# A hybrid decoder layer on one core: later x and row loads, pauses for the bias table, fewer convolution taps beside the first output projection

## The chip, the core and the metric

One core of a Trainium2 chip runs the whole layer as a single launch. The core has TensorE (PE: matrix products, with weight loads shown as PEld), VectorE (DVE), ScalarE (ACT), GpSimd (POOL) and SyncE (SP). SyncE does no arithmetic in this kernel: it issues nearly all transfers, in the order of its own instruction list. Each engine takes its instructions in the order in which the build wrote them, and an instruction whose inputs or buffer are not ready holds up all behind it on that engine. The metric is the device time of one execution in microseconds; lower is better.

## The reference

A decoder layer for 2048 tokens of width 1024 in float32. An input projection gives queries, keys and values of a sliding-window attention (8 query heads, 2 key heads, window 128, a learned sink per head, a relative-position bias from a table of 32 buckets) and the input of a convolution group (gate, causal depthwise convolution of width 31, LayerNorm, swish, pointwise product). Both go through one output projection; a SwiGLU channel mixer follows. RMSNorms stand before and after each half.

```python
hn = rms_norm(h, mix_pre_g)
proj = hn @ w_in
attn_out = sliding_window_attention(q, k, v, attn_sinks, rel_bias)
conv_out = conformer_conv(u, conv_dw, conv_dw_b, conv_ln_g, conv_ln_b, w_conv_pw)
mixed = jnp.concatenate([attn_out, conv_out], axis=-1) @ w_out
h = h + rms_norm(mixed, mix_post_g)
hn = rms_norm(h, ffn_pre_g)
ff = (jax.nn.silu(hn @ w_gate) * (hn @ w_up)) @ w_down
h = h + rms_norm(ff, ffn_post_g)
```

## The kernel before

The tokens are cut into four tiles of 512, held transposed (128 features by 512 tokens). Each float32 operand is split into a high part, rounded to fp32r, and the low remainder, and each product of 128x128 by 128x512 is done three times (high by high, high by low, low by high). ScalarE makes the high parts, VectorE or GpSimd the low ones.

**Stages and labels.** A tile's name in the profile carries the label of the stage that made it: A is the input projections, B attention, C the convolution, U the folding of pointwise and output weights, W the output projection with its norm, H the operands for the channel mixer, F its gate and up products in Strassen form (two tiles of 512 at a time), G its down products, X the bias table. The order in time is A0 (tile 0), A1, A2, A3 with W0 beside it, W1, F and G of the first half, in G also W2 and W3, then F and G of the second half.

**Input projection** (`stage_a`). A tile has 14 units; a unit loads one weight block of 512 KB into one of two `raw` buffers (line 137), ScalarE splits off the high part (line 127), GpSimd (units under 6 of tile 0) or VectorE the low part (line 129 or 94), and TensorE makes 24 products (line 85). Tile 0 also writes the low parts to HBM (line 131), and later tiles read them back (line 126). Six buffers `w`, two per unit, hold split weights. After a unit a *hook* may run, which emits work for the next tile: `load_x` loads its transposed x in four transfers of 512 KB (line 253), `row_norms` loads its rows (line 267: four of 512 KB for tile 1, eight for tiles 2 and 3 together), squares and sums them on ScalarE (line 268) and computes the reciprocal root on VectorE and GpSimd (lines 153 to 156); `norm_x` spreads that factor over the features (four scalings of the identity on VectorE, four transposes at line 302, a copy at line 304); `split_x` scales and splits x. In tile 0 the hooks are `load_x` after unit 2, `row_norms` after unit 4, `norm_x` after units 8 and 10, `split_x` after 11 and 12. In tile 1 they are `load_x` after 0, `row_norms` after 2, then 7, 9, 10, 11; in tile 2 `load_x` after 0, then 4, 7 and 11. Tile 0 gets its own norm through a product with ones and transposes between its units 2 and 3.

**Lanes.** The program text is one run of main stages; each `yield c` says that work of about c us was emitted. A planner (`Lane.pump`) gives each side stage a credit of c times the lane's rate and lets it emit its own steps while the credit lasts. So `lb` (bias table X, then attention) runs at 0.8, the taps `lc` at 0.7, 1.1 and 0.4 for tiles 0, 1 and 2 and 0.1 for tile 3 until the first half's G stage, then 0.9; a tap costs 0.68. `lw` runs W0 at 1.7 while A3 is emitted. Taps are held from the end of W1 until the channel mixer's operands S0 are there.

**Order.** The build orders each engine's list by priority and by its own estimate of when inputs are ready, so an instruction with free inputs may be put well ahead of its place in the text. A manual dependency of class `NoSync` draws an edge between two instructions for this ordering and adds no semaphore. Taps (`stage_taps`, one VectorE instruction per tap, 30 a chunk after the first, 4 chunks a tile) carry such edges to the last main VectorE instruction and to products; `made["rows"]` holds the products emitted since the last paced VectorE instruction asked for a new list. The differences of the down weights (`stage_tsums`) have the same edge written out by hand.

**Bias table** (`stage_x`). It loads the table and a one-hot matrix, multiplies them (a product of 32 rows), writes the result to HBM, pauses, loads a skewed copy of it, pauses, and flips it with two products into the tile that attention's softmax adds.

**Output projection** (`stage_w`). Per group of two inputs and per half of the columns, four blocks of products; VectorE adds each to the sum `x@W` (line 94), except in the first group. A block yields 1.3 for its two units, and there are 32; the lead is 4 and the norm's steps add up to 24.

**Handover to the second half.** `stage_pre` of F makes products whose partial sums go to HBM (`keeps`, line 980), come back into `gb` (line 943) and are copied into PSUM by ScalarE (line 959) ahead of the second products. The tail of the first half's G stage reads `h_scr` into `chl` in the same stretch.

Of the kernel before, what the change touches and what calls it, by code (L numbers as in the profile page):

```python
# [18 lines left out]
ALU = mybir.AluOpType  # L19
# [6 lines left out]
P = 128  # L26
T = 512
# [10 lines left out]
def layer_kernel(ctx, tc, x, xT, cols, rows, sinks, relb, onehot, w_in, w_pw, w_out, w_gate, w_up, w_down, out):  # L38
    nc = tc.nc
# [7 lines left out]
    lab = ["X0"]  # L47
# [7 lines left out]
    def t_(tag, shape, dt=F32):  # L55
        return sb.tile(list(shape), dt, tag=tag, name=nm(tag), bufs=BUFS[tag])

    def f4(tag, shape=(P, D)):
        return t_(tag, shape)

    def f2(tag, shape=(P, T)):
        return t_(tag, shape)
# [4 lines left out]
    def sm(n, dt=F32):  # L67
        kind = "A" if lab[0][0] == "G" else lab[0][0]
        return sb.tile([P, 8], dt, tag="sm" + kind, name=nm("sm"), bufs=16)[:, 0:n]
# [11 lines left out]
    pace = {"main": None, "tied": None}  # L81
    made = {"rows": [], "at": 0, "new": True}

    def mat(*args, **kw):
        r = nc.tensor.matmul(*args, **kw)  # L85
        if made["new"]:
            made.update(rows=[], at=0, new=False)
        made["rows"].append(r.ins)
        return r


    def dve(op):
        def emit(*args, **kw):
            r = op(*args, **kw)  # L94
            if not paced[0]:
                pace["main"] = r.ins
            elif pace["main"] is not None and pace["main"] is not pace["tied"]:
                tc.add_manual_dep(
                    r.ins,
                    pace["main"].name,  # L100
                    mybir.DependencyInfo(mybir.DependencyClass.NoSync, mybir.DependencyReason.DATA),
                    reason="conv taps keep pace with the projections",
                )
                pace["tied"] = pace["main"]
            if paced[0] and made["rows"]:
                made["new"] = True
                tc.add_manual_dep(
                    r.ins,
                    made["rows"][min(made["at"], len(made["rows"]) - 1)].name,
                    mybir.DependencyInfo(mybir.DependencyClass.NoSync, mybir.DependencyReason.DATA),  # L110
                    reason="conv taps keep pace with the products",
                )
                made["at"] += TIE
            return r

        return emit

    stt = dve(nc.vector.scalar_tensor_tensor)
    vtt = dve(nc.vector.tensor_tensor)
# [54 lines left out]
    def after_first(first, r, how="NoSync"):  # L174
# [4 lines left out]
            reason="products of half the array stand together",  # L179
        )  # L180

    def three(o, pairs, first=True, last=True):
        n = 3 * len(pairs)
        i = 0
        for (sh, sl), (mh, ml) in pairs:
            for a, b in ((sh, mh), (sh, ml), (sl, mh)):
                mat(o, a, b, start=first and i == 0, stop=last and i == n - 1)
                i += 1
# [12 lines left out]
    for i in range(4):  # L201
        xt = f4("x", (P, 2, T))
# [43 lines left out]
    started = set()  # L246

    def load_x(t):
        lab[0] = f"A{t}"
        xs = []  # L250
        for i in range(4):
            xt = f4("x", (P, 2, T))
            nc.sync.dma_start(xt, xT[2 * i : 2 * i + 2, :, t * T : (t + 1) * T].rearrange("c p t -> p c t"))
            xs.append(xt)
        started.add(f"x{t}")
        return [xs]
# [3 lines left out]
    def row_norms(ts, tag):  # L260
        lab[0] = f"A{ts[0]}"
        n = 4 * len(ts)
        ssq = sm(n)
        for i in range(n):
            xt = f4(tag)
            r0 = ts[0] * T + i * P
            nc.sync.dma_start(xt, x[r0 : r0 + P])
            act(junk, xt, AF.Square, accum_out=ssq[:, i : i + 1])
        r = rsqrt(ssq, n, D)
        for j, t in enumerate(ts):  # L270
            rn[t] = r[:, 4 * j : 4 * j + 4]
# [405 lines left out]
    def stage_x():  # L677
        lab[0] = "X0"
        rel = cst.tile([32, 8], F32, name="rel")
        nc.sync.dma_start(rel, relb)  # L680
        oh = f2("fa", (P, 2 * P))
        nc.sync.dma_start(oh[0:32], onehot)
        pb = tr()
        mat(pb[0:8, 0 : 2 * P], rel, oh[0:32], start=True, stop=True)
        bs = f2("fa", (P, 2 * P))
        nc.vector.tensor_copy(bs[0:8], pb[0:8, 0 : 2 * P])
        b_scr = dr.tile([8, 2 * P], F32, name="b_scr")
        nc.sync.dma_start(b_scr, bs[0:8])
        yield 8
        lab[0] = "X0"  # L690
        flip = f2("fa", (P, P))
        nc.gpsimd.memset(flip, 0.0)
        nc.gpsimd.affine_select(
            out=flip, in_=flip, compare_op=ALU.not_equal, fill=1.0, base=1 - P, pattern=[[1, P]], channel_multiplier=1
        )
        up = t_("mb", (P, 8, P))
        nc.sync.dma_start(up, bass.AP(tensor=b_scr.tensor, offset=b_scr.offset, ap=[[1, P], [2 * P, 8], [1, P]]))
        yield 8
        lab[0] = "X0"
        t = t_("mb", (P, 8, P))  # L700
        for n in range(2):
            o = tr()
            mat(o, flip, up[:, 4 * n : 4 * n + 4].rearrange("p h k -> p (h k)"), start=True, stop=True)
            nc.vector.tensor_copy(t[:, 4 * n : 4 * n + 4].rearrange("p h k -> p (h k)"), o)
        bias.append(t)
        yield 0.1
# [412 lines left out]
    def stage_tsums(td):  # L1119
        L = "G0"  # L1120
        for pr in range(NF // 2):
            lab[0] = L
            wx = f4("wx", (P, 2, T))
            b = [wx[:, 0], wx[:, 1], f2("fc"), f2("fc")]
            for i, (f, n) in enumerate(((0, 0), (0, 1), (1, 0), (1, 1))):
                nc.gpsimd.dma_start(b[i], w_down[2 * pr + f, :, n * T : (n + 1) * T])
            yield 3.9
            b11, b12, b21, b22 = b
            for to, o, p_, q_ in ((0, b11, b12, b11), (2, b12, b22, b12), (1, b22, b22, b11), (3, b21, b21, b22)):
                lab[0] = L  # L1130
                r = vtt(o, p_, q_, ALU.subtract)
                tc.add_manual_dep(
                    r.ins,
                    made["rows"][-1].name,
                    mybir.DependencyInfo(mybir.DependencyClass.NoSync, mybir.DependencyReason.DATA),
                    reason="weight differences keep pace with the products",
                )
                nc.gpsimd.dma_start(td[to, pr], o)
                yield 0.25

# [179 lines left out]
    class Lane:  # L1320
        def __init__(self, rate, lag):
            self.lag = lag
            self.rate = rate
            self.rates = {}
            self.items = []
            self.credit = 0.0
            self.done = {}
            self.hold = lambda: False

        def add(self, name, gen, needs=None):  # L1330
            self.items.append((name, gen, needs))

        def pump(self, dt):
            if self.hold():
                return
            self.credit = min(self.credit + dt * self.rate, 6.0)
            while self.items and self.credit > 0:
                name, gen, needs = self.items[0]
                self.rate = self.rates.get(name, self.rate)
                if needs and not needs():  # L1340
                    self.credit = 0.0
                    return
                p0 = tc.cur_priority
                tc.cur_priority = p0 + self.lag
                paced[0] = self.lag > 0
                try:
                    c = next(gen)
                    self.credit = 0.0 if c is None else self.credit - c
                except StopIteration:
                    self.done[name] = clk[0]  # L1350
                    self.items.pop(0)
                tc.cur_priority = p0
                paced[0] = False
# [32 lines left out]
    lc = Lane(RC0, LC)  # L1386
    lw = Lane(RW0, 0)
# [4 lines left out]
    ld = Lane(2.0, 0)  # L1392
    lanes = [lb, lc, lu, lw, ld, lf, lh, lt]
    lh.rates = {"N1": 1.2, "S0": 0.8, "B21.2": 0.5, "S2": 0.8}
    lf.rates = {n: 0.6 for n in ("O0.1", "O0.3", "E0.1", "E0.3")} | {n: 1.2 for n in ("Y0", "Y1", "O2.1", "O2.3")}
    lc.rates = {"T0": RC0, "T1": RC1, "T2": RC2, "T3": RP}
    lw.rates = {"W0": RW0, "C2": RW, "W2": RW, "C3": RW, "W3": RW}

    def run(gen):
# [60 lines left out]
    keeps = [dr.tile([PRES[2 * i], P, T], F32, name=f"keeps{i}") for i in range(2)]  # L1460
# [7 lines left out]
    lh.add("S0", stage_h_sums(ws, ops), lambda: "N1" in lh.done)  # L1468
    run(stage_pre(ws, ops, mids[0], keeps[0], Q0))
    lt.add("TS", stage_tsums(td))  # L1470
    run(stage_p1(ws, ops, mids[0], keeps[0]))
    lt.until("TS")
# [80 lines left out]
```

## Time and profile before

| | us |
|---|---|
| median of 3 runs | 1951.76 |
| lowest and highest run | 1948.69, 1952.41 |
| the profiled execution, its own time | 1951.41 |
| its span in the trace | 1949.7 |
| mean granted TensorE clock | 0.993 |

The page gives busy time per engine and the costliest groups. A row of the list in order of time has start, duration, engine, line, operation, the tile written, the tiles read, a count of instructions merged, and in brackets the idle time before it with what ended it. A row of the waits has the waiting engine and group, the releaser, total us, times and longest. A row of the stretches has start and end, length, then busy us with counts for PE, PEld, DVE, ACT and POOL, the granted TensorE clock, the DMA engines' busy share and GB/s. Tile names carry the stage's label after @.

### The profile page before, as it was taken

What the parts mean: (1) busy time and instruction counts of PE and PEld (TensorE: products, weight loads), DVE (VectorE), ACT (ScalarE), POOL (GpSimd) and SP (SyncE); (2) the same over time, 40 slices, a digit from 0 to 9 for tenths busy, and PEclk for the clock granted to TensorE, in tenths of its full rate; (3) what the DMA queues carried; (4) which work ended last, traced back from release to release, by engine and by line L of the source; (5) the groups of instructions that cost most, each with busy time, mean ns of one, the idle gap of its engine ahead of it and who ended that gap; (6) DMA issues with size and microseconds to landing.
All of it is one profiled execution on the core that took longest, in us unless ns stands there. A gap on an engine that the chain in (4) does not pass through costs nothing.

```text
span 1949.7 us, 26646 instructions
## 1 busy us (share of the span) xinstructions
PE 1902.9 (98%) x8730; PEld 1537.4 (79%) x8730; DVE 1475.9 (76%) x2648; ACT 958.6 (49%) x1886; POOL 299.0 (15%) x427
## 2 busy tenths in 40 slices
PE   8999999999999999999999999998999999999997
PEld 6777777777777787788888788886788888888886
DVE  4999979995986998888579945578677776465557
ACT  5355455457658433334353555476534333345453
POOL 4011021011120111120000100000032333211003
PEclk9999999999999999999999999998999999999998
DMA  8787667667758767676477876769645443375663
GB/s 308 250 309 229 220 209 236 199 206 237 245 199 288 269 227 257 241 269 228 144 272 240 315 249 206 237 235 362 216 159 162 154 154 103 124 252 185 206 199 141
DMA packets 209578, 435.67 MB, mean 223 GB/s; under 512 B 21752, under 2 KB 39328, under 8 KB 209440
## 3 DMA queue, kind: packets, MB, share of 16 engines
q1 hardware_dynamic: 191648, 402.52, 61.8%
q0 software_dynamic: 7040, 23.07, 3.4%
q10 hardware_dynamic: 10752, 8.39, 1.3%
q8 instruction: 68, 1.11, 0.2%
q14 instruction: 70, 0.57, 0.1%
HBM read 323.26 MB, written 110.63 MB: 223 GB/s over the span
## 4 chain that ended last, share of the span: by engine, by line
PE 67%; DVE 15%; DMA 10%; issue 4%; ACT 2%; POOL 2%; SPq 1%; DVEq 0%; POOLq 0%; ACTq 0%
PE mm@F L85 30%; PE mm@G L85 17%; PE mm@A L85 8%; DVE fc@C L94 5%; PE mm@W L85 4%; PE tr@W L85 3%; PE tr@B L85 2%; DMA mids<-fa@F 2%; DVE w@F L94 1%; DMA keeps<-fa@F 1%; DVE chl@F L94 1%; DVE fa@F L94 1%; DMA w@W<-fold 1%; DMA gb@F<-keeps 1%; PE tr@B L504 1%
## 5 line engine op out<-in xcount | busy, mean ns | idle before, releaser
L94 DVE SCALAR_TENSOR_TENSOR fc@C<-glu@C,colt,fc@C 128x512 f32<-128x512 f32 x480 | 359.0, 762 | 2.7
L85 PE MATMUL mm@F<-hl@H,w@F 128*128 128x512 f32 x1056 | 261.1, 398 | 14.8 <-ACT mm@F L959 13.6
L85 PEld LDWEIGHTS mm@F<-hl@H,w@F 128*128 128x128 f32 x1056 | 201.1, 192 | 61.6 <-ACT mm@F L959 17.7
L85 PE MATMUL mm@G<-hl@G,hl@G 128*128 128x512 f32 x924 | 227.4, 393 | 1.8 <-DVE hl@G L94 1.8
L841 ACT ACTIVATE w@F<-chl@F 128x512 fp32r<-128x512 f32 x220 | 136.3, 626 | 186.3 <-PE mm@F L85 164.8
L85 PE MATMUL mm@A<-hl@A,w@A 128*128 128x512 f32 x840 | 207.9, 395 | 4.0 <-ACT w@A L127 2.1
L85 PEld LDWEIGHTS mm@G<-hl@G,hl@G 128*128 128x128 f32 x924 | 171.6, 188 | 38.3 <-DVE hl@G L94 2.6
L85 PE MATMUL mm@G<-w@G,hl@G 128*128 128x512 f32 x876 | 199.4, 389 | 0.0
L94 DVE TENSOR_TENSOR w@F<-chl@F,w@F 128x512 fp32r<-128x512 f32 x198 | 151.0, 765 | 59.9 <-ACT w@F L841 59.7
L85 PEld LDWEIGHTS mm@G<-w@G,hl@G 128*128 128x128 f32 x876 | 164.5, 188 | 34.1
L85 PEld LDWEIGHTS mm@A<-hl@A,w@A 128*128 128x128 f32 x840 | 155.2, 188 | 43.2 <-issue 3.9
L85 PE MATMUL mm@F<-mid@H,w@F 128*128 128x512 f32 x528 | 132.7, 392 | 0.8 <-DVE fa@F L94 0.8
L85 PE MATMUL mm@F<-ql@H,w@F 128*128 128x512 f32 x528 | 130.1, 391 | 0.7 <-ACT w@F L841 0.7
L85 PE MATMUL mm@F<-p@H,w@F 128*128 128x512 f32 x528 | 129.1, 389 | 0.0
L85 PE MATMUL mm@F<-x@H,w@F 128*128 128x512 f32 x528 | 125.7, 391 | 0.0
L85 PEld LDWEIGHTS mm@F<-mid@H,w@F 128*128 128x128 f32 x528 | 99.8, 189 | 22.3 <-ACT at@F L1086 1.2
L85 PEld LDWEIGHTS mm@F<-x@H,w@F 128*128 128x128 f32 x528 | 98.7, 188 | 21.3 <-issue 0.8
L85 PEld LDWEIGHTS mm@F<-p@H,w@F 128*128 128x128 f32 x528 | 99.1, 188 | 20.6
L85 PEld LDWEIGHTS mm@F<-ql@H,w@F 128*128 128x128 f32 x528 | 98.5, 188 | 21.1 <-ACT w@F L841 1.1
L507 POOL TENSOR_SCALAR_AFFINE_SELECT p@B<-p@B 128x512 f32<-128x512 f32 x62 | 56.6, 918 | 338.1 <-ACT p@B L505 336.6
L127 ACT ACTIVATE w@A<-raw@A 128x512 fp32r<-128x512 f32 x110 | 67.4, 626 | 82.4 <-PE mm@A L85 50.3
L94 DVE TENSOR_TENSOR w@G<-raw@G,w@G 128x512 fp32r<-128x512 f32 x73 | 53.6, 734 | 71.7 <-ACT w@G L841 70.7
(316 smaller groups left out, 3240.0 us busy)
## 6 DMA issues: line engine op xcount, KB each, us to landing
mids<-fa@F SPq DMA_DIRECT2D x154, 256.0 KB, 3.0
raw@A<-w_in SPq DMA_DIRECT2D x55, 512.0 KB, 4.5
w@A<-lo_in SPq DMA_DIRECT2D x84, 256.0 KB, 3.8
fc@G<-mids SPq DMA_DIRECT2D x77, 256.0 KB, 3.4
fa@G<-mids SPq DMA_DIRECT2D x75, 256.0 KB, 4.5
gb@F<-keeps SPq DMA_DIRECT2D x72, 256.0 KB, 4.0
w@W<-fold SPq DMA_DIRECT2D x32, 512.0 KB, 5.7
chl@F<-w_gate SPq DMA_DIRECT2D x22, 512.0 KB, 4.8
```

The lines of the kernel that those rows point to most:

```text
L85: r = nc.tensor.matmul(*args, **kw)
L94: r = op(*args, **kw)
L127: act(w[:, 0], raw, AF.Copy)
L504: nc.tensor.transpose(o[:, i * P : (i + 1) * P], pr[:, 4 * g + i], ident)
L507: cut = nc.gpsimd.affine_select(out=pg[:, kb].rearrange("p (i q) -> p i q", q=P), in_=pg[:, 1].rearrange("p (i q) -> p i q", q=P), compare ...
L841: act(w[:, 0], x, AF.Copy)
```

## The change

A helper `tied` adds an order-only edge from an instruction to the last product emitted so far. The loads of x (`load_x`), the loads of rows (`row_norms`) and, as before but through the helper, the differences of the down weights get it. `stage_x` gains a pause of 6 between its first loads and its first product, and its last pause grows from 8 to 12. A lane gets a `share` that scales its credit; the taps' share is 0.6 from the start of A3 until W0 with its norm is done, once tile 0's convolution tail is through, else 1.

```diff
+    def tied(r):
+        tc.add_manual_dep(
+            r.ins,
+            made["rows"][-1].name,
+            mybir.DependencyInfo(mybir.DependencyClass.NoSync, mybir.DependencyReason.DATA),
+            reason="keeps pace with the products",
+        )
+        return r
...
-            nc.sync.dma_start(xt, xT[2 * i : 2 * i + 2, :, t * T : (t + 1) * T].rearrange("c p t -> p c t"))
+            tied(nc.sync.dma_start(xt, xT[2 * i : 2 * i + 2, :, t * T : (t + 1) * T].rearrange("c p t -> p c t")))
...
-            nc.sync.dma_start(xt, x[r0 : r0 + P])
+            tied(nc.sync.dma_start(xt, x[r0 : r0 + P]))
...
         nc.sync.dma_start(oh[0:32], onehot)
+        yield 6
+        lab[0] = "X0"
         pb = tr()
...
-        yield 8
+        yield 12
         lab[0] = "X0"
         t = t_("mb", (P, 8, P))
...
-                r = vtt(o, p_, q_, ALU.subtract)
-                tc.add_manual_dep(
...
-                )
+                tied(vtt(o, p_, q_, ALU.subtract))
...
+            self.share = lambda: 1.0
...
-            self.credit = min(self.credit + dt * self.rate, 6.0)
+            self.credit = min(self.credit + dt * self.rate * self.share(), 6.0)
...
+    lc.share = lambda: 0.6 if "A3" in started and "C0" in ld.done and "W0" not in lw.done else 1.0
```

More of the change, by code (lines that the diff above doesn't have):

```diff
@@ L1130, in stage_tsums @@
                 lab[0] = L
-                r = vtt(o, p_, q_, ALU.subtract)
-                tc.add_manual_dep(
[L1133 to L1136, printed above, removed]
-                )
+                tied(vtt(o, p_, q_, ALU.subtract))
                 nc.gpsimd.dma_start(td[to, pr], o)
```

## The prediction

> **What bounds the kernel now.** I read the page first, then busy time by stage, then who waited for whom on TensorE, and then the lists in order of time around each wait that the change touches. The page:
>
> ```profile
> span 1949.7 us, 26646 instructions
> PE 1902.9 (98%) x8730; PEld 1537.4 (79%) x8730; DVE 1475.9 (76%) x2648; ACT 958.6 (49%) x1886; POOL 299.0 (15%) x427
> ```
>
> TensorE is the bound: 1949.7 - 1902.9 leaves 46.8 us without a product. The change removes no product, so all it can win lies in those 46.8 us, and it matters where they are. Busy time by stage (us of the stretch, then PE, PEld, DVE, ACT, POOL, granted clock, DMA share and GB/s; tile 0's projections, tile 1's, tile 2's, tile 3's with the first output projection, the Strassen steps of the first half, the handover to the second half, the tail):
>
> ```profile
> 0.00:98.00 98.00, 91.04 (x401) 72.84 (x402) 71.94 (x131) 44.51 (x72) 24.53 (x37) 1.00 0.82 279
> 98.00:193.00 95.00, 93.86 (x492) 74.00 (x491) 91.39 (x222) 54.47 (x145) 10.96 (x20) 1.00 0.78 268
> 193.00:318.00 125.00, 124.66 (x629) 94.81 (x629) 108.93 (x244) 66.17 (x162) 19.61 (x30) 1.00 0.70 224
> 318.00:471.00 153.00, 149.72 (x751) 114.88 (x750) 134.30 (x295) 79.19 (x184) 25.80 (x58) 1.00 0.68 218
> 653.00:930.00 277.00, 270.54 (x1180) 221.43 (x1179) 243.65 (x393) 106.71 (x187) 45.32 (x84) 0.99 0.72 242
> 1275.00:1375.00 100.00, 87.94 (x375) 70.40 (x374) 85.56 (x192) 69.48 (x137) 0.00 (x0) 0.94 0.88 312
> 1937.00:1950.00 13.00, 0.48 (x3) 0.06 (x1) 8.94 (x31) 0.69 (x2) 0.00 (x0) 0.61 0.31 121
> ```
>
> Stretch less PE gives the idle time: 6.96, 1.14, 0.34, 3.28, 6.46, 12.06 and 12.52 us. The first four are where the change works, 11.72 us in all; the fifth and sixth are where its delayed taps end up; the last it cannot reach. TensorE's waits in tile 0 (20 to 75 us) and in the output projection (330 to 450 us), with total, times and longest:
>
> ```profile
> PE mm@A L85 <- ACT w@A L127: 1.9, 1, 1.9
> PE tr@X L85 <- DMA mb@X<-b_scr: 1.1, 1, 1.1
> PE mm@A L85 <- POOL w@A L129: 0.6, 1, 0.6
> PE tr@X L85 <- DMA fa@X<-onehot: 0.2, 1, 0.2
> ...
> PE mm@W L85 <- DVE x@W L94: 2.1, 1, 2.1
> PE mm@A L85 <- DVE x@W L94: 0.7, 1, 0.7
> PE mm@W L85 <- DVE fa@A L94: 0.3, 1, 0.3
> ```
>
> **Part 1: x and rows of tile 1.** Their hooks stand after units 2 and 4 of tile 0, yet SyncE issues them from 11.89 us on (start, duration, line, count):
>
> ```profile
> 11.89 0.38 SPq L253 DMA_DIRECT2D x@A<-xT  x1
> ...
> 13.19 0.34 SPq L267 DMA_DIRECT2D p@A<-x  x1
> ...
> 21.63 0.33 SPq L137 DMA_DIRECT2D raw@A<-w_in  x1
> ...
> x@A<-xT SPq DMA_DIRECT2D x4, 512.0 KB, 9.5
> p@A<-x SPq DMA_DIRECT2D x4, 512.0 KB, 9.2
> ```
>
> The last two rows are the DMA view of 9 to 22 us (count, size, median us to landing): 8 transfers of 512 KB, 4 MB, ahead of the weight of unit 3 (the issue at 21.63). The DMA view of 20 to 30 us, then the weight loads of 9 to 75 us (time to landing), then ScalarE and TensorE in order of time:
>
> ```profile
> DMA packets 1625, 4.06 MB, mean 406 GB/s; under 512 B 144, under 2 KB 144, under 8 KB 1624
> ...
> raw@A<-w_in SPq DMA_DIRECT2D x2, 512.0 KB, 8.8
> ...
> DMA to landing us min/median/max: 3.8/5.5/10.0
> ...
> 30.55 0.60 ACT L304 ACTIVATE gb@A<-ct@A 128x512 f32<-128x512 f32 x1 [2.81 <-PE ct@A L302]
> 31.75 1.15 ACT L127 ACTIVATE w@A<-raw@A 128x512 fp32r<-128x512 f32 x2 [0.61 <-POOL sm@A L156]
> ...
> 32.44 0.73 PE L85 MATMUL mm@A<-hl@A,w@A 128*128 128x512 f32 x2 [1.93 <-ACT w@A L127]
> 33.80 11.40 PE L85 MATMUL mm@A<-hl@A,w@A 128*128 128x512 f32 x49 [0.62 <-POOL w@A L129]
> ```
>
> The transfer engines are full and a weight takes up to 10.0 us where 3.8 is the least. 21.63 + 10.0 = 31.63, just before ScalarE's split of unit 3 at 31.75: TensorE's 1.93 us are the price of that landing. The 0.62 us behind it is GpSimd's low part, late for the same reason. With the 4 MB behind products of units 2 and 4 (about 30 and 44 us: unit 3 starts at 32.44, and 24 of the 49 products at 33.80 take 5.6), the weight lands 3.8 to 5.5 us after issue, by 27, and both waits go: **-1.93 - 0.62 = -2.55**. Upper bounds: if ScalarE still takes unit 3 behind the copy at L304, only 31.75 - 31.15 = 0.6 is won; and the 4 MB move, they don't vanish: 2 MB ahead of the weight of unit 5 or 6 cost 2 / 0.406 = 5 us of queue, so the other end is +5.0. I take -2.55, because each of the two parcels is half of what delayed unit 3 and the weights then are two units ahead.
>
> The Trainium skill, "DMA: Bandwidth & Descriptors", section "Rules for kernel authors", speaks against this part: issue a DMA early and wait on its semaphore late. By it the time would be that of the rival "rows late" below; the 8.8 us landing above shows the other side, that an early load takes the queue from a more urgent one.
>
> **Part 2: x of tiles 2 and 3, rows of both.** These 16 transfers move behind units 0 and 2 of tile 1 and unit 0 of tile 2. TensorE lost 1.14 us in tile 1's stretch and 0.34 in tile 2's. I cost it at 0, hidden by the projections of the four or more units between load and use; bounds -1.5 (both losses go) and +1.9 (one more wait like unit 3's, if that cover is too short). SyncE's queue behind them holds the low halves of tile 1's weights; nothing else is moved past.
>
> **Part 3: pauses for the bias.** The table's products wait twice for a transfer, 1.1 and 0.2 us in the list above. A unit of 5.2 gives this lane 5.2 x 0.8 = 4.2, so the new pause of 6 puts the first product one or two units behind its loads, and 12 in place of 8 makes it three units instead of two for the shifted copy. One unit, 5.6 us, covers both waits: **-1.3** (bounds -1.3 to 0). A loss is excluded: the products end up near the end of unit 9 (44 + 5 x 5.6 = 72 us), and attention's first product comes at 106:
>
> ```profile
> 106.12 0.97 PE L85 MATMUL tr@B<-kz,ql@A 64*128 64x256 f32 x12
> ```
>
> **Part 4: fewer taps.** The lane of tile 2 runs at 0.4 and costs 0.68 a tap. The output projection's steps add up to 4 + 32 x 1.3 + 24 = 70, at its lane's 1.7 that is 41 of the planner's us. So 41 x 0.4 x 0.4 / 0.68 = about 10 taps are left out there and come later. VectorE between 318 and 437 us, and in order of time ahead of the longest wait:
>
> ```profile
> L94 DVE SCALAR_TENSOR_TENSOR fc@C<-glu@C,colt,fc@C 128x512 f32<-128x512 f32 x89 | 66.0, 770 | 0.1
> ...
> 381.47 1.40 DVE L94 SCALAR_TENSOR_TENSOR fc@C<-glu@C,colt,fc@C 128x512 f32<-128x512 f32 x2
> ...
> 384.01 1.65 PE L85 MATMUL mm@W<-w@W,hl@W 128*128 128x512 f32 x6 [2.15 <-DVE x@W L94]
> ```
>
> Two taps (1.40) stand straight ahead of the sum that TensorE waits 2.15 for. VectorE is full here, and 10 of 89 taps give it back 10 x 0.77 = 7.7 us. That can take at most 0.30 + 0.69 + 2.15 = 3.14 from TensorE; only 41 x 0.4 / 0.68 = 24 of the 89 are emitted there, the other 65 are left over from earlier and stay, so I take half: **-1.6** (bounds -3.14 to 0).
>
> The ten come back at 0.4: 10 x 0.68 / 0.4 = 17 us more of tile 2's taps in the Strassen steps, and tile 3, at 0.1 meanwhile, loses 17 x 0.1 / 0.68 = 2.5 taps, made up at 0.9 later in 2 us. There VectorE is 88% busy (243.65 of 277) and TensorE loses 6.46 / 277 = 0.023 a us: 17 x 0.023 = **+0.4** (bounds 0 to +2.3, the longest wait there):
>
> ```profile
> 672.71 2.36 PE L85 MATMUL mm@F<-yt@H,w@F 128*128 128x512 f32 x6 [2.29 <-DVE at@F L94]
> ```
>
> **The sum.** The profiled execution took 1951.41 us, 1.7 more than its span; the median of the runs is 1951.76. -2.55 - 1.3 - 1.6 + 0.4 = -5.05 on 1951.41 gives **1946.4 us**, 0.27% under the median.
>
> **The rivals.** *The handover pays (slower).* TensorE's waits of 1300 to 1380 us, and the chain there:
>
> ```profile
> PE mm@F L85 <- ACT mm@F L959: 12.1, 5, 5.1
> ...
> 1326.60 8.57 DMA chl@G<-h_scr
> ...
> 1335.24 5.76 DMA keeps<-fa@F
> ...
> 1346.41 6.60 DMA gb@F<-keeps
> ```
>
> Five products wait for sums that go out to HBM and come back through SyncE's one queue, behind loads of h. Tile 3's taps end 2 us later, its output projection and norm follow, and whatever then falls into that queue ahead of a sum costs a round trip. Two more waits of 5.1 are +10.2: 1956.6. For it: 12.06 us are lost there already, with DMA at 88%. Against it: 2 us is little against the 145 us from the last tap (1130) to there:
>
> ```profile
> L94 DVE SCALAR_TENSOR_TENSOR fc@C<-glu@C,colt,fc@C x480: 692/744/1777, 46.2 to 1130.0; 128x512 f32<-128x512 f32 x160
> ```
>
> It decides from a second extra wait on; one alone (1951.5) would be no change. *The handover gains.* The same lottery with one wait of 5.1 less: 1941.3. *The collision.* Part 1 ends at its +5.0: 1946.4 + 7.55 = 1953.9. For it: unit 6's weight has no slack now, ScalarE waits 6.66 us for it. *Rows late.* The rows' way from issue to the factor's use on VectorE:
>
> ```profile
> 47.27 1.16 ACT L127 ACTIVATE w@A<-raw@A 128x512 fp32r<-128x512 f32 x2 [6.66 <-DMA raw@A<-w_in]
> ...
> 45.45 0.89 DVE L94 TENSOR_SCALAR gb@A<-ident,sm@A 128x128 f32<-128x128 f32 x4
> ```
>
> is 45.45 - 13.19 = 32.3 us. From 44 that ends at 76, while the hook after unit 8 asks near 66: 10 us in which VectorE stands, and the weight splits behind it. Two units of prepared weights cover some of it; uncovered it is 1956.4. Against it: most of the 32.3 was queueing on a full DMA and behind GpSimd's low parts, which end with unit 5. *It does not do what it says.* The loads' landing still sits behind L304 (-0.6 for part 1) and the 65 left-over taps keep VectorE full (0 for part 4): 1951.41 - 0.6 - 1.3 + 0.4 = 1949.9.
>
> **How the numbers follow.** Forecast 0.48, its own range 1943 to 1949; handover pays 0.19; it does not do what it says 0.12; collision 0.08; handover gains 0.08; rows late 0.05. What a measurement of this kernel can tell from no change is about 0.2%, 3.9 us, so faster means under 1947.9 and slower over 1955.7. Faster: 0.40 of the forecast and the gaining handover, 0.48. Slower: the paying handover, rows late, and 0.01 of the collision, 0.25. The same: the rest, 0.27. The range goes from the gaining handover to just past the paying one, 1941 to 1957.
>
> **What would show it.** Part 1: no x or row load of tile 1 ahead of unit 3's weight, that weight landing in under 6 us, tile 0's stretch with 2.5 us less idle; a TensorE wait at units 5 to 7 would be the collision, a VectorE wait for the factor near 66 us rows late. Part 3: no wait before the table's products. Part 4: about 79 taps where there were 89, and under 2 us lost to VectorE. The handover: its 12.06 us within 3. If the handover moves by more than the first four stretches do, the prediction is wrong whatever its sum.

## The result, and the profile after

| | before | after |
|---|---|---|
| median of the runs, us | 1950.7 (4 runs, 1948.69 to 1952.41) | 1973.07 (4 runs, 1970.41 to 1973.63) |
| the profiled execution, its own time | 1951.41 | 1973.63 |
| its span | 1949.7 | 1971.7 |

The ratio after to before is 1.0112, 95% interval 1.0095 to 1.013: the kernel became 22 us slower, outside the range given. First the page of the changed kernel, then the tile views of both kernels: of each group of products the shortest, median and longest duration in ns, and the first start and the last end of the group.

```profile
span 1971.7 us, 26622 instructions
PE 1912.3 (97%) x8730; PEld 1539.2 (78%) x8730; DVE 1479.3 (75%) x2648; ACT 958.7 (49%) x1886; POOL 301.7 (15%) x427
```

```profile
L85 PE MATMUL mm@A<-mid@A,w@A x336: 387/389/505, 98.3 to 467.3; 128*128 128x512 f32 x168
L85 PE MATMUL mm@A<-chl@A,w@A x168: 387/389/499, 101.5 to 192.6; 128*128 128x512 f32 x168
L85 PE MATMUL mm@A<-hl@A,w@A x840: 387/389/792, 8.2 to 470.5; 128*128 128x512 f32 x168
L85 PE MATMUL mm@F<-mb@H,w@F x264: 387/389/396, 655.3 to 1732.2; 128*128 128x512 f32 x132
```

```profile
L85 PE MATMUL mm@A<-mid@A,w@A x336: 387/390/796, 104.6 to 485.7; 128*128 128x512 f32 x168
L85 PE MATMUL mm@A<-chl@A,w@A x168: 387/390/628, 107.8 to 206.2; 128*128 128x512 f32 x168
L85 PE MATMUL mm@A<-hl@A,w@A x840: 387/390/796, 7.0 to 488.4; 128*128 128x512 f32 x168
L85 PE MATMUL mm@F<-mb@H,w@F x264: 388/389/397, 672.9 to 1754.1; 128*128 128x512 f32 x132
```

The same 8730 products, 9.4 us more busy (1912.3 - 1902.9) and 12.6 us more without one (22.0 of span less 9.4). The operands' names date the loss. `mid` is first read in tile 1, so its first start is the end of tile 0's projections: 98.3, now 104.6, **+6.3**. `chl` is last read at the end of tile 1: 192.6, now 206.2, **+7.3 more**. The last `hl` ends tile 3: 470.5, now 488.4, **+4.3**. The last `mb` product lies near the end of the gate and up products of the second half: 1732.2, now 1754.1, **+4.0**; after it nothing is added. 13.6 of 22 us are lost before tile 2 begins.

**Tile 0.** The list in order of time of the changed kernel, SyncE's issues and then ScalarE and TensorE (its L262 and L276, the loads of x and rows, are L253 and L267 of the kernel before):

```profile
28.19 2.03 SPq L262 DMA_DIRECT2D x@A<-xT  x4
...
34.87 0.33 SPq L137 DMA_DIRECT2D raw@A<-w_in  x1
43.17 0.32 SPq L131 DMA_DIRECT2D lo_in<-w@A  x1
...
44.79 1.85 SPq L276 DMA_DIRECT2D p@A<-x  x4
...
51.27 1.62 SPq L137 DMA_DIRECT2D raw@A<-w_in  x2
...
59.04 1.15 ACT L127 ACTIVATE w@A<-raw@A 128x512 fp32r<-128x512 f32 x2 [4.04 <-DMA raw@A<-w_in]
...
59.72 1.22 PE L85 MATMUL mm@A<-hl@A,w@A 128*128 128x512 f32 x2 [5.06 <-ACT w@A L127]
61.28 1.22 PE L85 MATMUL mm@A<-hl@A,w@A 128*128 128x512 f32 x2 [0.34 <-ACT w@A L127]
63.03 6.89 PE L85 MATMUL mm@A<-hl@A,w@A 128*128 128x512 f32 x22 [0.53 <-DVE w@A L94]
```

The wait of 1.93 us at unit 3 is gone, as predicted. But SyncE stands from 35.2 to 43.17 for a low half of unit 5, whose weight was issued behind the four x, at 32.16, and split only 9.0 us later. Only behind that low half does SyncE issue the four rows (2 MB); the weights of units 7 and 8 come behind these, at 51.27, and the first is split 7.8 us after its issue. TensorE waits 5.06 us, then 0.34 and 0.53, and runs slowly behind: 22 products in 6.89 us.

**Tile 1.** The last row before which TensorE stands, and the same place in the kernel before:

```profile
190.35 5.49 PE L85 MATMUL mm@A<-mid@A,w@A 128*128 128x512 f32 x12 [5.84 <-DVE ql@A L94]
```

```profile
174.32 3.02 PE L85 MATMUL mm@A<-mid@A,w@A 128*128 128x512 f32 x12
177.17 2.88 PE L85 MATMUL mm@A<-chl@A,w@A 128*128 128x512 f32 x12
179.90 2.92 PE L85 MATMUL mm@A<-mid@A,w@A 128*128 128x512 f32 x12
...
179.06 0.67 DVE L94 SCALAR_TENSOR_TENSOR ql@A<-mm@A,ql@A 128x512 fp32r<-128x512 f32 x1
```

TensorE needs a PSUM bank (one of its output buffers) that VectorE empties with the subtraction `ql@A`. That stands behind the operations that scale and split x of tile 2: all 16 of them in the kernel before, 15 in the changed one, with three taps and two more operations of attention among them. From the first of them to the start of the subtraction it takes 10.8 us before and 14.0 after. In the kernel before, that subtraction ended at 179.06 + 0.67 = 179.73 and the product that needed it began at 179.90: no wait, and 0.17 us to spare. In the changed kernel it ends 10.6 us later, and TensorE has stood for 5.84 us by then.

### The profile page after: what moved, and what is told of

Read it like the earlier page. It is cut to its first block, busy times and chain, and to the rows that moved or that the text cites. A ratio compares the mean times of both kernels' runs of the same rounds, so it can differ in the third digit from the quotient of the medians.

```text
span 1971.7 us, 26622 instructions
## 1 busy us (share of the span) xinstructions
PE 1912.3 (97%) x8730; PEld 1539.2 (78%) x8730; DVE 1479.3 (75%) x2648; ACT 958.7 (49%) x1886; POOL 301.7 (15%) x427
## 4 chain that ended last, share of the span: by engine, by line
PE 68%; DVE 13%; DMA 10%; issue 3%; ACT 3%; POOL 2%; SPq 1%; DVEq 0%; POOLq 0%; ACTq 0%
PE mm@F L85 27%; PE mm@G L85 18%; PE mm@A L85 10%; DVE fc@C L94 4%; PE tr@W L85 4%; PE mm@W L85 4%; DMA mids<-fa@F 3%; PE tr@B L85 2%; DVE w@F L94 1%; DMA raw@F<-w_gate 1%; PE mm@U L85 1%; DVE chl@F L94 1%; DVE fa@F L94 1%; DMA gb@F<-keeps 1%; PE tr@B L513 1%
```

## The experiments

All are cut from the changed kernel. Ratios are to the kernel before on the same chip, timed beside it (its medians there lay between 1954 and 1956 us, so ratios are compared, not times). The columns in between are read as above, in each profiled execution, against the profile of before: end of tile 0, end of tile 1, and TensorE's wait for `ql@A`. The paced kernel before ran twice: the two ends agreed within 0.4 us, while its last `mb` product came 2.0 us earlier than in before the first time and 4.8 us later the second. What one profile says of the second half is uncertain by as much. Nor does an end that moves in tile 1 always reach the total: with the loads of tiles 2 and 3 tied it moves by 3.8 us and the total does not.

| kernel | tile 0 | tile 1 | wait | ratio, 95% interval |
|---|---|---|---|---|
| ties alone | -1.8 | +4.5 | 4.1 | 1.0006 (0.9994 to 1.0018) |
| pauses alone | -0.4 | +1.4 | 1.4 | 1.0011 (1.0002 to 1.0021) |
| fewer taps alone | +0.6 | +0.4 | 0 | 1.0023 (1.0011 to 1.0035) |
| pauses and fewer taps | -0.6 | +0.3 | 0 | 1.0024 (1.0015 to 1.0034) |
| ties and pauses | +5.4 | +10.6 | 4.9 | 1.0086 (1.0062 to 1.011) |
| ties and fewer taps | -1.4 | +5.5 | 4.1 | 1.0063 (1.004 to 1.0085) |
| the change, all three | +6.3 | +13.6 | 5.8 | 1.0112 (1.0095 to 1.013) |
| only x tied | -3.7 | +4.6 | 6.4 | 1.0022 (1.0006 to 1.0037) |
| only rows tied | -1.0 | +6.8 | 6.1 | 1.0063 (1.0041 to 1.0085) |
| only tile 1's loads tied | -1.7 | +8.6 | 6.9 | 1.0046 (1.0026 to 1.0065) |
| only tiles 2's and 3's tied | -0.4 | +3.8 | 3.8 | 0.9986 (0.9971 to 1.0002) |
| the change, tile 1's rows free | -3.7 | +3.0 | 5.1 | 1.0044 (1.003 to 1.0058) |
| ties, taps slowed in tile 1 | -1.9 | +6.6 | 7.5 | 1.0021 (1.0003 to 1.0038) |
| before, paced | -0.5 | -1.8 | 0 | 0.9979 (0.9964 to 0.9994) |
| the same again | -0.9 | -1.5 | 0 | 0.9986 (0.9975 to 0.9998) |
| tile 1's x tied, paced | -3.7 | -3.1 | 0.4 | 1.0026 (1.0008 to 1.0044) |
| ties, paced | +1.7 | +5.3 | 3.5 | 1.0071 (1.0048 to 1.0094) |
| the change, paced | +5.8 | +4.5 | 0 | 1.008 (1.0053 to 1.0108) |
| the change, rows free, paced | -3.7 | -5.2 | 0 | 1.0024 (1.0013 to 1.0035) |

"Paced" means that taps are emitted at 0.85 of their pace until tile 2 begins.

**One edit at a time.** Each run keeps one edit, the fourth two, and undoes the rest by these lines:

```diff
-            tied(nc.sync.dma_start(xt, x...))
+            nc.sync.dma_start(xt, x...)
...
-        yield 6
...
-        yield 12
+        yield 8
...
-    lc.share = lambda: 0.6 if "A3" in started ...
+    lc.share = lambda: 1.0 if "A3" in started ...
```

> Only the ties of x and of the rows are kept; the bias has its old pauses and the taps of tile 2 their old pace beside the first output projection. Theory (the ties alone cost the time: 2 MB of x and 2 MB of rows stand ahead of tile 0's weights of units 6 to 8, and in tile 1 the splits of x fall among the taps): nearly all of the loss stays, 1968 to 1975 us, with a TensorE wait of about 5 us for the split weight near 60 us and one near 185 to 190 us for x or its split. Rival A (the delayed taps cost it): within 1947 to 1954. Rival B (the pauses of the bias cost it): within 1947 to 1954 as well; the two runs beside this one tell A from B.

> Only the two pauses of the bias are changed. Theory (ties): 1949 to 1951.5 us, the two waits of 1.1 and 0.2 us for the bias's transfers gone and nothing else. Rival B (pauses): 1960 or more. Rival A (taps): no change, as the theory says.

> Only the taps beside the first output projection are slowed. Theory (ties): 1948 to 1953 us, a stretch from 318 to 471 us that is 0 to 3 us shorter and a handover to the second half that moves by less than 4 us. Rival A (taps): 1960 or more, with the added idle time behind 1275 us.

> The changed kernel without the ties of x and rows: the pauses and the slower taps together. Theory (ties): the sum of the two runs before this one, 1946 to 1952 us. Rival C (any change of order in this kernel shifts the time by some us, whatever it is meant to do): the sum does not hold by more than 4 us.

My first theory, that the ties alone cost the time, fell: with the ties alone there is no difference clear of noise. The three single effects add to 0.06 + 0.11 + 0.23 = 0.40%, and together they cost 1.12%; 0.7%, some 14 us, exist only in combination. Tile 0 says where. With the ties alone:

```profile
35.29 4.61 SPq L276 DMA_DIRECT2D p@A<-x  x4
...
48.66 0.84 SPq L137 DMA_DIRECT2D raw@A<-w_in  x2
...
55.10 0.73 PE L85 MATMUL mm@A<-hl@A,w@A 128*128 128x512 f32 x2 [0.64 <-ACT w@A L127]
```

The rows are issued at 35.29 here, 9.5 us sooner than in the change (44.79), while SyncE would otherwise stand. The next weights leave at 48.66 instead of 51.27, and the wait is 0.64 instead of 5.06: tile 0 wins 1.8 us. The slower taps alone did not shorten the longest wait that they were to shorten, still 2.1 us: 84 taps stand there instead of 89, where 79 were forecast. The stretch of tile 3 and the first output projection, for which the prediction showed 149.72 us of products in before, is in this run

```profile
318.00:471.00 153.00, 149.72 (x743) 114.58 (x742) 134.71 (x294) 77.47 (x181) 26.83 (x58) 0.99 0.68 214
```

As busy as before, with 8 products fewer on record. From the end of tile 1 to the end of tile 3 it takes 472.2 - 193.0 = 279.2 us, where before took 470.5 - 192.6 = 277.9.

**Two edits, and one kind of load at a time.** The first two restore the old taps or the old pauses; the other two take one tie out of the ties alone.

> Ties and pauses together, the taps at their old pace. Theory (the pauses move tile 1's rows behind low halves of weights in SyncE's queue: issued at 44.8 us in the changed kernel, at 35.3 us with the ties alone; the weights of units 7 and 8 then queue behind those 2 MB): rows issued near 45 us, a TensorE wait of about 5 us for a split weight near 60 us, the end of tile 0's projections 6 to 8 us later than with the ties alone, and 8 to 16 us over before in all. Rival (the three edits act apart from one another): the sum of the runs with one edit, +1.4 and +2.5, about 4 us over before and no wait near 60 us.

> Ties and slower taps together, the bias with its old pauses. Theory: tile 0 as with the ties alone (rows near 35 us, no wait of 5 us near 60 us), tile 1 with its wait of 4 to 6 us for a split of x, the rest as with the slower taps: 3 to 9 us over before. Rival (the ties and the slower taps are what loses together): 15 us or more over before.

> Only the loads of x are tied, not the rows. Theory for tile 1 (taps get between the splits of x because the rows and x of tile 2 come 18 to 26 us later): if x is what is late, the wait of about 4 us for the split of x stays in tile 1 (end of tile 1's projections 4 to 6 us behind tile 0's end as against before); if the rows are, it goes. In tile 0 the unit 3 wait of 1.9 us is halved or gone.

> Only the rows are tied, not x. The counterpart: if the rows are what is late, the wait of about 4 us for the split of x stays in tile 1; if x is, it goes and the time is within 3 us of before. In tile 0 2 MB of x still stand ahead of unit 3's weight, so 0.6 to 1.9 us of its wait stay.

Ties with pauses bring the rows back to 43.84 us and TensorE's wait to 5.13 us: the collision needs both edits. Each kind of tie by itself has tile 1's wait, so neither x nor the rows alone are to blame. Ties with fewer taps follow the ties alone up to tile 1, as expected, but lose 0.63%, more than the 0.29% of the sum; where that arises was not found.

**Which tile's loads, and the rows alone.**

```diff
+            r = nc.sync.dma_start(xt, x...)
+            if t == 1:
+                tied(r)
```

for tile 1's loads alone (`t > 1` for the others), the rows likewise; the third is the change with the rows of tile 1 untied; the fourth is the ties alone with

```diff
+    lc.share = lambda: 0.85 if "A1" in started and "A2" not in started else 1.0
```

> Only tile 1's x and rows are tied (the loads of tile 0's stage); tiles 2 and 3 load as before, old pauses, old taps. Theory (tile 1 loses because the late x and rows of tile 2 let more taps run on VectorE ahead of its splits of x): tile 0's projections end 1 to 4 us earlier than in before, tile 1's wait of 4 to 6 us for the split goes, its projections take no longer than before, and the time is 1 to 5 us under before. Rival (VectorE is the bound of tile 1, busy 91.39 of 95 us in before, so that what tile 0 wins is lost there in any case): tile 1's projections end within 1 us of before, with the wait in it.

> Only the loads for tiles 2 and 3 are tied; tile 1's load as before. Theory: tile 0 as before within 1 us, a TensorE wait of 4 to 6 us for a split of x in tile 1, its projections 5 to 8 us longer than before, with 65 to 70 taps ahead of that split where before had 60. Rival (VectorE as the bound): no more than 2 us longer, since nothing is won in tile 0.

> The changed kernel with one thing undone: the four rows of tile 1 are not tied. Theory (with the pauses those rows fall behind the waiting low halves in SyncE's queue and then stand ahead of the weights of units 7 and 8): the wait of 5 us near 60 us goes, tile 0's projections end 2 to 4 us before those of before, where the changed kernel ends them 6.3 us behind; tile 1 keeps its loss of 5 to 8 us; in all 8 to 14 us under the changed kernel. Rival (the pauses themselves put the bias's transfers in the way): the wait near 60 us stays at 3 us or more.

> All ties as in the run with the ties alone, and the taps emitted at 0.85 of their pace during tile 1's projections. Theory (taps ahead of the splits of x are what TensorE waits for): 58 to 62 taps ahead of that split where the ties alone had 67, the wait of 4.1 us is at most 1.5, tile 1's projections take 3 to 6 us less than with the ties alone; the taps left over may cost some of it later. Rival (the splits are late because x or its factor lands late, not because of taps): the wait stays at 3 us or more.

With tile 1's rows untied, the change has its rows out ahead of everything urgent and no wait near 60 us:

```profile
12.55 2.14 SPq L276 DMA_DIRECT2D p@A<-x  x4
...
25.43 2.31 SPq L262 DMA_DIRECT2D x@A<-xT  x4
```

Tile 0 ends 3.7 us early instead of 6.3 late: this one tie costs the change 10.0 us there. In tile 1 both theories failed in their simple form: the wait comes with tile 1's ties alone (6.9 us) and with the later ones alone (3.8). Slowing the taps only in tile 1 made it 7.5: 68 taps still ran ahead of the release, where 58 to 62 were expected, presumably because they had been emitted before. VectorE from 60 us to its release of TensorE, in before, in the change, with tile 1's loads tied and with the later loads tied (the third number after the length is VectorE's busy time):

```profile
60.00:179.73 119.73, 117.92 (x586) 93.59 (x586) 116.42 (x247) 61.62 (x145) 9.46 (x18) 1.00 0.75 254
```

```profile
60.00:190.35 130.35, 123.64 (x596) 97.00 (x596) 121.85 (x256) 64.16 (x150) 9.34 (x23) 0.97 0.72 249
```

```profile
60.00:185.69 125.69, 117.26 (x579) 92.13 (x577) 119.95 (x251) 62.81 (x146) 10.37 (x18) 0.99 0.76 258
```

```profile
60.00:182.44 122.44, 118.39 (x588) 93.58 (x587) 116.41 (x246) 62.99 (x146) 7.62 (x18) 1.00 0.74 250
```

VectorE is nearly full in all four: it idles 3.3, 8.5, 5.7 and 6.0 us. In the change it has 5.4 us more to do ahead of the release and 5.2 us more idle, which is its 10.6 us. With tile 1's loads tied it is 3.5 and 2.4; with the later loads tied the work is the same to 0.01 us and the 2.7 us of later release are idle time alone. With tile 1's loads tied the extra work is taps. In the change only 1.8 us of the 5.4 are; 2.5 us are low parts of weights that VectorE splits behind 60 us, 14 in place of 10, because the weights of units 7 and 8 land late. In before and in the change, behind 60 us:

```profile
L94 DVE TENSOR_TENSOR w@A<-raw@A,w@A 128x512 fp32r<-128x512 f32 x10 | 6.8, 684 | 0.3 <-ACT w@A L127 0.3
```

```profile
L94 DVE TENSOR_TENSOR w@A<-raw@A,w@A 128x512 fp32r<-128x512 f32 x14 | 9.3, 685 | 0.1
```

The taps between the end of tile 0 and the release, in before, in the change and with tile 1's loads tied:

```profile
L94 DVE SCALAR_TENSOR_TENSOR fc@C<-glu@C,colt,fc@C 128x512 f32<-128x512 f32 x60 | 44.4, 752 | 0.6
```

```profile
L94 DVE SCALAR_TENSOR_TENSOR fc@C<-glu@C,colt,fc@C 128x512 f32<-128x512 f32 x65 | 47.8, 761 | 0.5
```

```profile
L94 DVE SCALAR_TENSOR_TENSOR fc@C<-glu@C,colt,fc@C 128x512 f32<-128x512 f32 x71 | 52.0, 763 | 0.3
```

Fewer taps have run by the end of tile 0, and part of the rest stands ahead of the release in tile 1: 34 and then 60 in before, 26 and 65 in the change, 20 and 67 with the ties alone, 20 and 71 here. That a shorter tile 0, or one in which VectorE stands longer, runs fewer taps is a reading of these counts; it was not tried by itself.

**Taking VectorE's work away.** If VectorE bounds the two tiles, moving taps out of them must free TensorE:

```diff
+    lc.share = lambda: 0.85 if "A2" not in started else 1.0
```

(in the change: 0.85 until tile 2 begins, then as it was).

> The kernel before, with the taps emitted at 0.85 of their pace until tile 2 begins (83 taps ahead of the split of x in tile 1 instead of 98). Theory (VectorE bounds tiles 0 and 1 together): TensorE did not wait there in before, so tile 0 and tile 1 end within 1.5 us of before, and the 15 taps, 11 us of VectorE, cost 0 to 5 us in tiles 2 and 3 or the first output projection. It is the yardstick for the next three.

> Only the four loads of tile 1's x are tied, and the taps run at 0.85 until tile 2 begins. Theory (VectorE as the bound): tile 0 ends 3 to 4 us before that of before, no wait for a split of x over 1.5 us in tile 1, so that tile 1 ends 3 to 5 us earlier than in before, and the time is 2 to 5 us under the run before this one. Rival (late loads): as tile 2's loads are as in before, it says the same; the next run tells them apart.

> All ties, old pauses, taps at 0.85 until tile 2 begins. Theory (VectorE as the bound): the wait of 4.1 us for the split of x goes (1.5 us at most stay), tile 1 ends 1 to 4 us earlier than in before, where with the ties alone it ended 4.5 us later. Rival (x and rows of tile 2 come too late): the wait stays at 3 us or more, tile 1 ends 3 us or more later than in before.

> The changed kernel with the taps at 0.85 until tile 2 begins. Theory (two causes: rows ahead of weights in tile 0, VectorE as the bound of tile 1): tile 0 still ends 5 to 7 us behind before with its wait near 60 us, the wait of 5.8 us in tile 1 goes, and tile 1 ends 4 to 8 us behind before instead of 13.6; the time is 3 to 9 us under the changed kernel. Rival (late loads): tile 1 still ends 11 us or more behind before.

> The changed kernel with both causes taken out: tile 1's rows untied and the taps at 0.85 of their pace until tile 2 begins. Theory: no wait of 5 us near 60 us, at most 1.5 us for the split of x in tile 1; tile 0 ends 3 to 4 us and tile 1 2 to 6 us before that of before, where the changed kernel ends them 6.3 and 13.6 us behind. Behind tile 1 the earlier runs with paced taps lost 4 to 12 us to the end of the first output projection and the second half, so the whole should come out 2 us under to 8 us over before. Rival (a third cause in tiles 0 and 1): tile 1 ends later than in before.

> The kernel before with the taps at 0.85 of their pace until tile 2 begins, a second time. If the first result holds: a ratio of 0.997 to 0.9995 to the kernel before, 1 to 6 us faster; if it was scatter: an interval that has 1.000 in it.

In the paced change, VectorE and TensorE up to the product in question, and the product itself:

```profile
60.00:184.28 124.28, 123.07 (x594) 96.92 (x594) 113.98 (x245) 62.51 (x146) 9.48 (x21) 0.98 0.76 254
```

```profile
184.33 3.02 PE L85 MATMUL mm@A<-mid@A,w@A 128*128 128x512 f32 x12
```

VectorE now has 10.3 us to spare, the wait of 5.84 us is gone, and tile 1 ends 4.5 us behind before instead of 13.6. With the rows free as well both losses are gone: tile 0 ends 3.7 us and tile 1 5.2 us before that of before. Tile 1 thus ends 18.8 us earlier than in the change, and the ratio falls by 0.88%, some 17 us, where the same pacing alone gave the kernel before 0.14 to 0.21%: most of the loss of the whole hangs on these two. The ties with paced taps are the miss: 60 taps ahead of the release, as in before, and still 3.49 us of wait; VectorE is busy 114.25 of 123.57 us there, so that idle time stands where taps were. Loads that are issued later are thus a second, smaller cause. They do not act by landing too late. In the run with the later loads tied, x of tile 2 is issued from 125.19 us on, lands a median 9.3 us later, and VectorE takes it up only at 169.51. The trace points to ScalarE: it squares the eight rows between 121.33 and 136.94 us, among attention's exponentials, which begin at 124.42; in before the squares are done at 118.33 and the exponentials begin at 119.89. VectorE then waits for attention's sums, twice between 98 and 183 us, where in before it does not:

```profile
DVE sm@B L94 <- ACT sm@B L496: 1.7, 1, 1.7
...
DVE sm@B L94 <- ACT p@B L499: 0.9, 1, 0.9
```

These 2.6 us are nearly all of the 2.7 us of idle time above. In the paced ties such waits are 4.4 us. Tile 0 also came out at +1.7 in that run, with a wait of 1.73 us for a weight; the reason was not found.

The kernel before with paced taps is the only version whose interval lies under 1: 0.9979 and, the second time, 0.9986 (0.9975 to 0.9998), 3 to 4 us. With tile 1's x tied besides, both tiles end earlier as expected, but the whole is 0.26% over before, where 2 to 5 us under the paced kernel before were expected. That early finish is lost again later, and so is the one with both causes out. Waits of the Strassen steps of the first half, before and with both out, in stretches of 328 and 339 us:

```profile
PE mm@F L85 <- DVE at@F L94: 3.7, 2, 2.3
...
PE mm@F L85 <- DVE fa@F L94: 0.8, 1, 0.8
```

```profile
PE mm@F L85 <- DVE at@F L94: 7.2, 6, 2.3
PE mm@F L85 <- DVE fa@F L94: 4.4, 1, 4.4
```

```profile
L94 DVE SCALAR_TENSOR_TENSOR fc@C<-glu@C,colt,fc@C 128x512 f32<-128x512 f32 x68 | 50.4, 742 | 0.0
```

```profile
L94 DVE SCALAR_TENSOR_TENSOR fc@C<-glu@C,colt,fc@C 128x512 f32<-128x512 f32 x86 | 63.4, 743 | 0.0
```

The last two rows are the taps in those stretches: 68 before, 86 now. The waits for VectorE's sums rise by 3.5 and 3.6 us with them. That these taps are the cause was not tried by itself.

## Why the prediction was wrong

**Part 1, -2.55: the wait went, the forecast of what follows failed.** Both waits at unit 3 behaved as worked out (1.93 gone; 0.62 us of waiting for a low part came again at 43.20). With x alone moved, tile 0 won 3.7 us, with x and rows 1.8. The 3.7 are the forecast 2.55 and the bias's two waits, 1.28, which went with x alone and without a pause: for x Part 1 was right, and it left Part 3 nothing to win. The step that failed is the choice between the ends: "I take -2.55, because each of the two parcels is half of what delayed unit 3 and the weights then are two units ahead". The weights were not two units ahead. The rows fell behind a waiting low half in SyncE's list, and in front of the weights of units 7 and 8. That is the collision rival, with its 2 MB, which had 0.08; it came at unit 7, where the rival named unit 6. That its 5 us of queue and the measured wait of 5.06 agree is luck: against the ties alone, unit 7's weight leaves 2.6 us later and takes 2.0 us longer from issue to split. The tie of the rows was shown to carry 10.0 us of the change's tile 0.

**Part 2, 0 with a bound of +1.9: mis-sized.** "Hidden by the projections of the four or more units" looked at TensorE's cover and not at VectorE, which the prediction's own row showed busy for 91.39 of 95 us in tile 1. The later loads alone cost tile 1 4.2 us (from -0.4 to +3.8), through VectorE's waits for attention and the slow clock behind TensorE's, although the kernel as a whole then came out equal to before (0.9986, interval to 1.0002). With tile 1's loads the loss in tile 1 was 10.3 us. A wait by VectorE for late rows was in the rival "rows late", at unit 8 of tile 0. The change has it, sooner:

```profile
55.03 0.58 DVE L94 TENSOR_SCALAR sm@A<-sm@A 128x4 f32<-128x4 f32 x3 [4.57 <-ACT junk L277]
```

But TensorE's 5.06 us ended on a weight and not on VectorE. The rule of the Trainium skill that Part 1 quotes, to issue early and wait late, holds for the rows of tile 1: issued at 12.55 they cost tile 0 nothing. For x it does not: x tied alone, and so issued later, gave tile 0 its 3.7 us.

**Part 3, -1.3, "a loss is excluded": wrong.** The two waits for the bias went, but tile 0 won 0.4 us with the pauses alone, where the wait at unit 3 came out longer (2.44 us) and the 49 products behind it took 1.0 us more at a slow clock. Alone the pauses made the kernel 0.11% slower (0.02 to 0.21). Their real cost is in Part 1: they move tile 1's rows in SyncE's list. I added the parts as if each order were its own; the build makes one order from all.

**Part 4, -1.6 and +0.4: both mis-sized.** There was no gain (279.2 us from the end of tile 1 to that of tile 3, where before took 277.9): half as many taps left the stretch as forecast, and its longest wait stayed. The slower taps alone cost 0.23% (0.11 to 0.35), about 4.5 us, where later costs of 0.4 were forecast with a bound of 2.3.

**The clock was left out of every term.** A stall was priced at its own length. TensorE's granted clock in the change, around the wait of tile 0 and behind that of tile 1:

```profile
60.00:63.00 3.00, 2.17 (x4) 0.72 (x4) 2.17 (x7) 1.75 (x4) 0.93 (x5) 0.50 0.44 137
...
190.00:194.00 4.00, 3.65 (x9) 2.88 (x10) 3.96 (x14) 0.00 (x0) 0.00 (x0) 0.50 0.00 0
194.00:198.00 4.00, 4.00 (x15) 3.17 (x14) 0.45 (x1) 0.63 (x1) 0.00 (x0) 0.73 0.55 129
198.00:202.00 4.00, 4.00 (x31) 3.23 (x30) 3.75 (x7) 3.10 (x6) 0.25 (x1) 1.00 0.58 184
```

Half the clock from 190 to 194 us and, by the 0.73, for some 2 more; so the way from the release to the end of tile 1 takes 206.2 - 190.35 = 15.85 us where it took 192.6 - 179.73 = 12.9: 3 us on top of the 5.84. Tile 1's 7.3 us are thus: VectorE's release 10.6 later, less the 6.3 by which tile 0 had already been late, plus 3.0. The Trainium skill, "TensorE: Matmul & The Clock Gate", section "What's actually happening", has this: after an idle window of about 3.4 us the array runs at half clock until it has been busy for about as long. The trace agrees on the half clock, at 0.50 after 5.06 and 5.84 us. The slow stretch is longer here, some 6 us, and other runs show one behind shorter waits (last section).

**The handover** did not decide: its waits came to 13.5 us where before had 12.1, and all that came behind tile 3 added 4.0 us, where its rival had 10.2. The forecast looked for loss there and at the waits of one stage; the 14 us that exist only in combination had no term.

**Left open:** the 4.3 us of tiles 2 and 3 in the change (one new wait stands there, 3.1 us for VectorE's `sm@B` at 399 us; its reason was not found), what the fewer taps cost when alone, the further loss of ties with fewer taps, and why the build puts the rows behind the low half once the pauses are there: SyncE's list shows that it does, not the reason.

## What to carry to other kernels

When a wait on the bounding engine is removed, look for the next engine that is nearly full in the following stage: if it has the same work to do by a certain point, the wait can come back there, and idle time given to that engine comes on top. Before moving a load, list what stands ahead of and behind it in its queue after all edits of the change, since edits that are harmless alone share one order. Price a stall of TensorE with the slow clock that can follow it: here 1.6 to 3 us on top of waits of 3.5 us and more, and in some executions 1.5 us on top of two short ones.

## What the runs showed of the hardware

A slow clock can follow when TensorE stands, and the length of the wait alone does not say what it costs. Behind the wait for `ql@A` an undisturbed dozen of products takes 2.88 us. It took 3.06 behind 1.38 us (the pauses alone), and 4.5 to 5.5 behind 3.5 to 7.5 us, in no order of length: 4.51 with the ties alone, 5.43 behind the same wait with ties and fewer taps, and 4.91 behind the longest, 7.53.

```profile
181.11 3.06 PE L85 MATMUL mm@A<-mid@A,w@A 128*128 128x512 f32 x12 [1.38 <-DVE ql@A L94]
```

```profile
182.38 4.51 PE L85 MATMUL mm@A<-mid@A,w@A 128*128 128x512 f32 x12 [4.05 <-DVE ql@A L94]
```

```profile
182.50 5.43 PE L85 MATMUL mm@A<-mid@A,w@A 128*128 128x512 f32 x12 [4.06 <-DVE ql@A L94]
```

Short waits can have it too. At unit 3 of tile 0 TensorE waits 1.93 and 0.62 us in before, and 1.51 and 0.62 with the fewer taps alone, an edit that sets in only with tile 3. The 49 products behind these waits took 11.40 us in before and here

```profile
33.43 12.88 PE L85 MATMUL mm@A<-hl@A,w@A 128*128 128x512 f32 x49 [0.62 <-POOL w@A L129]
```

The stretch from 34 to 36 us, in before and with the fewer taps alone, has the clock at 1.00 and at 0.50:

```profile
34.00:36.00 2.00, 2.00 (x10) 1.62 (x10) 0.75 (x2) 1.02 (x2) 2.00 (x3) 1.00 0.37 144
```

```profile
34.00:36.00 2.00, 2.00 (x6) 1.59 (x5) 0.39 (x1) 1.38 (x3) 2.00 (x3) 0.50 0.58 226
```

So 1.5 us went behind the shorter wait and none behind the longer. Of the seven profiles in which tile 1's loads are not tied, four have the slow clock there. The ends of tile 0 in the table that differ by 1 to 2 us may differ by this alone.
